# The feed-forward part of a two-layer encoder: inner features in three parts, and more of its products from half blocks

## The chip, the cores and the metric

The kernel runs on one core of one Trainium2 chip. The number that counts is the device time of one execution in microseconds. A core has a matrix engine (TensorE, PE in the profile; PEld is its weight load), an elementwise engine (VectorE, DVE), a scalar and activation engine (ScalarE, ACT), GpSimd (POOL), and SyncE (SP), whose queue issues most transfers from main memory.

## The reference

The program is an encoder of two layers over 512 tokens of 1024 features. The part of a layer that the change touches is the last line of the loop:

```python
    for layer in range(DEPTH):
        ...
        x = x + merged @ w_o[layer]
        h = rmsnorm(x, ffn_norm[layer])
        x = x + (jax.nn.silu(h @ w_gate[layer]) * (h @ w_up[layer])) @ w_down[layer]
    return rmsnorm(x, final_norm)
```

`w_gate` and `w_up` are 1024 x 2816, `w_down` is 2816 x 1024. The 2816 inner features are 22 blocks of 128.

## The kernel before

**Products in three.** All large products are made in a 32-bit format of reduced precision (`F32R`), with each float32 operand split into a rounded value `hi` and the rest `lo`. `mm3` (L207 to L210) adds hi x hi, hi x lo and lo x hi into one bank. A weight is split by `wsplit`: ACT casts (L92 as the profile names it) and DVE subtracts (L81). The results live in `hi` and `lo` tiles of 1024 columns, three of each (`hp`). The raw weight comes through `wload` (L193) into two buffers `raw` of 1 MB.

**Features across partitions.** xT (the residual stream) and hh/hl (the two halves of the normed input) hold features on the 128 partitions, 8 tiles of 512 tokens each. One block of 128 inner features is 8 x 3 = 24 matmuls of 512 columns into one bank `m`, times rbc (the rms scale of each token) on the way out. The blocks go in 11 pairs: gate block and up block of the pair, silu (gate) x up, split into gh/gl, which hold all 22 blocks.

**Seven products.** For 7 of the 11 pairs (blocks 4 to 17) the up pair is made by `seven`: the 256 outputs by 512 tokens by 1024 features of two blocks are cut in halves in each direction, 2 x 2 x 2, and seven products of half blocks (12 matmuls of 256 columns each) take the place of eight, after the scheme of Strassen and Winograd. The mixed weights (`sw`, s1, s2, a21 in place) are made on DVE as the call goes, the mixed inputs once per layer by `combine`, into `com` and into the space of gh/gl that is not in use yet. The products arrive in banks `m` and `y` and are summed into `u` (`gu` in rows).

**Back to 1024 features.** After the 11 pairs come the products with `w_down`: in layer 0 two output tiles at a time, each 22 blocks of 3 matmuls in one bank, summed into xT and absorbed into the next layer's hh/hl; in layer 1 with tokens on the partitions, eight banks open at once and the blocks in the outer loop, after xT has been transposed (L990) for the final norm.

**What sets the order.** Each engine takes its instructions in the order written by the build. Pieces inside `urgent()` (a priority) are moved ahead of the rest on their engine as far as buffers allow, so that splits of the next block run while PE is at this one. A tile of a pool with few buffers makes its next writer wait for its last reader.

Of the kernel before, what the change touches and what calls it, by code (L numbers as in the profile page):

```python
# [18 lines left out]
P = 128  # L19
# [28 lines left out]
def kernel(  # L48
# [679 lines left out]
    for l in range(LAYERS):  # L728
# [106 lines left out]
        with tc.tile_pool(name=f"ffn{l}", bufs=2, reuse_waits="tile") as fp:  # L835
            gh = fp.tile([P, FC, T], F32R, name="gh", bufs=1)
            gl = fp.tile([P, FC, T], F32R, name="gl", bufs=1)
# [3 lines left out]
            own = [fp.tile([P, DC // 2, 2, T // 2], F32R, name=name, bufs=1) for name in ("comh", "coml")]  # L841
            half = lambda v: v.rearrange("p (h t) -> p h t", h=2)
            spare = [v[:, FC - 4:FC, :].rearrange("p k (h t) -> p k h t", h=2) for v in (gh, gl)]
            com = lambda part, i, k: (spare if i < 2 else own)[part][:, k, i % 2, :]

            def combine(k):

                ge, go = an[2 * k], an[2 * k + 1]
                (x11, x12), (x21, x22) = [[half(xT[:, c, :])[:, i, :] for i in range(2)] for c in (2 * k, 2 * k + 1)]
                d, e = [half(fp.tile([P, T], F32, tag=tag, name="com", bufs=1)) for tag in ("s1", "s2")]  # L850
                u, v, m, n = d[:, 0, :], d[:, 1, :], e[:, 0, :], e[:, 1, :]
# [9 lines left out]
            def pair_of(tag):  # L861
                return fp.tile([P, 2, T], F32, tag=tag, name="gu", bufs=1)

            def tile_of(raw):

                with urgent():
                    wh, wl = wsplit(raw)
                ps = mbank()
                for c in range(DC):
                    mm3(ps, wh[:, c, :], wl[:, c, :], hh[:, c, :], hl[:, c, :], c == 0, c == DC - 1)  # L870
                return ps

            def gate(s, raw):
                ps = tile_of(raw)
                with urgent():
                    tt(s, ps, rbc, ALU.mult)
                    return act(s, s, AF.Silu)

            def seven(rg, ru, f0):

                s, u = pair_of("gu0"), pair_of("gu1")
                quarter = u.rearrange("p f (h t) -> p (f h) t", h=2)
                blk = lambda i, j: ru.rearrange("p (k two) c -> p k two c", two=2)[:, :, j, i * P:(i + 1) * P]
                a11, a12, a21, a22 = blk(0, 0), blk(0, 1), blk(1, 0), blk(1, 1)
                s1, s2 = [fp.tile([P, T], F32, tag=tag, name="sw", bufs=1).rearrange("p (k c) -> p k c", c=P)
                          for tag in ("s1", "s2")]

                def two():
                    return [hp.tile([P, 1024], F32R, tag=tag, name=tag).rearrange("p (h k c) -> p h k c", h=2, c=P)
                            for tag in ("hi", "lo")]  # L890
# [7 lines left out]
                mixed = lambda i: lambda part, k: com(part, i, k)  # L898
                of = lambda v, h: lambda part, k: v[part][:, h, k, :]
# [12 lines left out]
                product(p1, lambda part, k: first[part][:, 2 * k, :], plain(0, 0))  # L912
                with urgent():
                    ACT.copy(quarter[:, 1, :], p1)
                product(b26[:, 0, :], lambda part, k: first[part][:, 2 * k + 1, :], plain(1, 0))
                with urgent():
                    third = two()
                    split_act(s1, third[0][:, 0], third[1][:, 0])
                    split_act(a22, third[0][:, 1], third[1][:, 1])
                product(b26[:, 1, :], of(second, 0), mixed(1))  # L920
                with urgent():
                    tt(quarter[:, 0::3, :], quarter[:, 1:2, :].to_broadcast([P, 2, T // 2]), b26, ALU.add)
                    tt(s2, a12, s2, ALU.subtract)
                    fourth = two()
                    split_act(s2, fourth[0][:, 0], fourth[1][:, 0])
                product(b57[:, 1, :], of(second, 1), mixed(2))
                product(b57[:, 0, :], of(third, 0), mixed(0))
# [3 lines left out]
                product(b34[:, 1, :], of(third, 1), mixed(3))  # L931
                product(b34[:, 0, :], of(fourth, 0), plain(1, 1))
# [3 lines left out]
                with urgent():  # L936
                    tt(s, s, rbc.unsqueeze(1).to_broadcast([P, 2, T]), ALU.mult)
                    tt(u, u, s, ALU.mult)
                    split_act(u, gh[:, f0:f0 + 2, :], gl[:, f0:f0 + 2, :])
                return silu  # L940

            for f0 in range(0, FC, 2):
                with urgent():
                    rg = wload(rows(w_gate[l], 0, DC, f0 * P, 256))
                    ru = wload(rows(w_up[l], 0, DC, f0 * P, 256))
                if 4 <= f0 < FC - 4:
                    last_silu = seven(rg, ru, f0)
                    continue
                s, u = pair_of("gu0"), pair_of("gu1")
                for i in range(2):  # L950
                    if f0 + i < DC // 2:
                        combine(f0 + i)
                    last_silu = gate(s[:, i, :], rg[:, :, i * P:(i + 1) * P])
                    ps = tile_of(ru[:, :, i * P:(i + 1) * P])
                    with urgent():
                        tt(u[:, i, :], ps, rbc, ALU.mult)
                        tt(u[:, i, :], u[:, i, :], s[:, i, :], ALU.mult)
                        split_act(u[:, i, :], gh[:, f0 + i, :], gl[:, f0 + i, :])
            with tc.issue_after(last_silu.ins):
                lnexp = ACT.preload_act_table_set("natural_log_exp_and_others")  # L960
            groups = [(0, 8), (8, 8), (16, 6)]
            if l < LAYERS - 1:
                nn = [vecs[:, V_ATT + 8 * (l + 1) + c:V_ATT + 8 * (l + 1) + c + 1] for c in range(DC)]
                for c0 in range(0, DC, 2):
                    ps = [mbank(), mbank()]
                    for k0, nk in groups:
                        with urgent():
                            raw = wload(rows(w_down[l], k0, nk, c0 * P, 256))
                        for j in range(2):
                            with urgent():  # L970
                                wh, wl = wsplit(raw[:, :, j * P:(j + 1) * P])
                            for k in range(nk):
# [98 lines left out]
```

## Time and profile before

| | |
|---|---|
| time of the kernel, median of 3 runs | 1609.79 us (1609.61 to 1610.27) |
| the profiled execution's own time, its span | 1612.3 us, 1610.6 us |
| granted clock of TensorE, mean | 0.998 |
| busy: PE, PEld, DVE, ACT | 1595.3, 1342.1, 1122.2, 814.2 us |
| data moved, mean rate | 142.63 MB, 89 GB/s |

The profile comes from one execution, 1612.3 us, of which the trace covers 1610.6. A matmul's listed duration is longer than the time to the next one's start, since they overlap; what a stream of them costs is read from start to start. An engine's busy time counts overlapped work once.

### The profile page before, as it was taken

Reading aid. Unit: us, or ns where it says so; the run is one execution under the profiler, and the core shown is the slowest. Engines: PE = TensorE matmul, PEld = TensorE weight load, DVE = VectorE, ACT = ScalarE, POOL = GpSimd, SP = SyncE. Lnnn points to the kernel's source line nnn. Section 1 sums busy time; section 2 is a strip of 40 time slices with the busy share of each in tenths; the row PEclk is TensorE's granted clock in tenths of the full one; section 3 lists DMA queues with packets and bytes.
Section 4 is the critical chain, followed back from the end, with each engine's and each line's share of the span. In section 5 each row is a group of like instructions: output and inputs, shape, how many; then the busy total and the mean of one; then the engine's idle time right before and its main releaser. Section 6 shows DMA issues by size and latency. Waiting matters only on the chain.

```text
span 1610.6 us, 20117 instructions
## 1 busy us (share of the span) xinstructions
PE 1595.3 (99%) x7977; PEld 1342.1 (83%) x7977; DVE 1122.2 (70%) x1827; ACT 814.2 (51%) x1292; POOL 8.0 (0%) x21
## 2 busy tenths in 40 slices
PE   9999999999999999999999999999999999999998
PEld 7788888887888999888888888888878899988886
DVE  8888968887676777533368789788876767774224
ACT  4666665686453344322255567676754534343213
POOL 1000000000000000000000000000000000000000
PEclk9999999999999999999999999999999999999999
DMA  5312212221322333322332221213122332242321
GB/s 190 105 53 79 79 53 79 78 80 36 122 81 77 105 105 105 107 90 98 99 104 79 79 79 61 71 55 103 53 79 79 105 105 89 96 128 95 105 84 73
DMA packets 118078, 142.63 MB, mean 89 GB/s; under 512 B 3168, under 2 KB 100704, under 8 KB 117984
## 3 DMA queue, kind: packets, MB, share of 16 engines
q1 hardware_dynamic: 117696, 141.05, 26.8%
q8 instruction: 63, 1.03, 0.3%
q10 hardware_dynamic: 288, 0.30, 0.1%
q14 instruction: 31, 0.25, 0.0%
HBM read 139.23 MB, written 2.10 MB: 88 GB/s over the span
## 4 chain that ended last, share of the span: by engine, by line
PE 85%; DVE 9%; ACT 4%; issue 1%; DMA 1%; SPq 0%; DVEq 0%; ACTq 0%
PE m L209 21%; PE m L210 21%; PE m L208 21%; PE y L210 3%; PE y L209 3%; PE y L208 3%; DVE lo L81 2%; PE sc L549 2%; DVE fl L81 2%; PE s L209 1%; PE s L208 1%; PE s L210 1%; PE qk L666 1%; ACT hi L92 1%; DVE z L81 1%
## 5 line engine op out<-in xcount | busy, mean ns | idle before, releaser
L92 ACT CAST hi<-raw 128x1024 fp32r<-128x1024 f32 (+2 forms) x288 | 274.5, 954 | 496.3 <-PE m L209 251.6
L81 DVE TENSOR_TENSOR lo<-raw,hi 128x1024 fp32r<-128x1024 f32 (+2 forms) x296 | 322.9, 1092 | 219.6 <-ACT hi L92 218.8
L208 PE MATMUL m<-hh,hi 128*128 128x512 f32 (+1 forms) x1048 | 404.4, 386 | 1.2 <-DVE hi L296 1.1
L210 PE MATMUL m<-hh,lo 128*128 128x512 f32 (+1 forms) x1048 | 403.9, 386 | 0.0
L209 PE MATMUL m<-hl,hi 128*128 128x512 f32 (+1 forms) x1048 | 403.6, 385 | 0.0
L208 PEld LDWEIGHTS m<-hh,hi 128*128 128x128 f32 x1048 | 197.5, 189 | 40.2 <-ACT sq L78 1.5
L210 PEld LDWEIGHTS m<-hh,lo 128*128 128x128 f32 x1048 | 197.0, 188 | 38.4 <-DVE lo L81 0.2
L209 PEld LDWEIGHTS m<-hl,hi 128*128 128x128 f32 x1048 | 197.1, 188 | 38.0
L208 PE MATMUL m<-hi,hh 128*128 128x512 f32 x256 | 101.7, 397 | 0.0
L209 PE MATMUL m<-lo,hh 128*128 128x512 f32 x256 | 101.1, 395 | 0.0
L210 PE MATMUL m<-hi,hl 128*128 128x512 f32 x256 | 100.9, 394 | 0.0
L81 DVE TENSOR_TENSOR gu<-m,rbc 128x512 f32<-128x512 f32 x60 | 41.3, 689 | 61.7 <-PE m L210 60.6
L78 ACT ACTIVATE fl<-fl 128x1024 f32<-128x1024 f32 (+1 forms) x56 | 48.5, 872 | 41.8 <-DVE fl L81 41.8
L210 PE MATMUL m<-gh,lo 128*128 128x512 f32 x176 | 68.5, 389 | 0.0
L208 PE MATMUL m<-gh,hi 128*128 128x512 f32 x176 | 68.5, 389 | 0.0
L209 PE MATMUL m<-gl,hi 128*128 128x512 f32 x176 | 68.5, 389 | 0.0
L210 PEld LDWEIGHTS m<-hi,hl 128*128 128x128 f32 x256 | 48.3, 189 | 9.6
L208 PEld LDWEIGHTS m<-hi,hh 128*128 128x128 f32 x256 | 48.3, 189 | 9.4
L549 PEld LDWEIGHTS sc<-fl 128*128 128x128 f32 x384 | 50.0, 194 | 7.3 <-issue 2.6
L209 PEld LDWEIGHTS m<-lo,hh 128*128 128x128 f32 x256 | 48.3, 189 | 9.3
L549 PE MATMUL sc<-fl 128*128 128x128 f32 x384 | 52.2, 279 | 1.9 <-DVE fl L81 1.8
L92 ACT CAST gh<-gu 128x512 fp32r<-128x512 f32 (+1 forms) x30 | 24.7, 822 | 56.6 <-DVE gu L81 56.5
(293 smaller groups left out, 3047.1 us busy)
## 6 DMA issues: line engine op xcount, KB each, us to landing
raw<-in_w_in_dram SPq DMA_DIRECT2D x46, 1024.0 KB, 5.0
raw<-in_w_gate_dram SPq DMA_DIRECT2D x22, 1024.0 KB, 5.1
raw<-in_w_up_dram SPq DMA_DIRECT2D x22, 1024.0 KB, 5.1
raw<-in_w_down_dram SPq DMA_DIRECT2D x19, 1024.0 KB, 4.8
raw<-in_w_o_dram SPq DMA_DIRECT2D x8, 1024.0 KB, 4.7
raw<-in_w_b_dram SPq DMA_DIRECT2D x4, 1024.0 KB, 4.9
raw<-in_w_a_dram SPq DMA_DIRECT2D x4, 1024.0 KB, 5.0
raw<-in_w_down_dram SPq DMA_DIRECT2D x4, 768.0 KB, 4.1
```

Source lines behind the costliest of these rows:

```text
L78: return ACT.activation(o, i, func, **kw)
L81: return DVE.tensor_tensor(o, a, b, op)
L92: return ACT.copy(hi, src), tt(lo, src, hi.bitcast(F32), ALU.subtract)
L208: PE.matmul(ps, lh, rh, start=start, stop=False)
L209: PE.matmul(ps, lh, rl, start=False, stop=False)
L210: PE.matmul(ps, ll, rh, start=False, stop=stop)
L549: mm = PE.matmul(ps[:, c], K[:, c], Q[:, c], start=True, stop=True)
L666: PE.matmul(ps[c], q2[:, c, tok], kb[:, c, :], start=False, stop=True)
```

## The change

- The 22 inner blocks come in three parts of 8, 8 and 6 (`parts`). gh/gl become tiles of 8 blocks, two of each in turn.
- The products of `w_down` with one part are written as a generator (`down`), which makes one output tile (8 x 3 matmuls) at a time. While the next part's gate and up pairs are made, `next(todo)` puts one or two of these tiles after each of them, and `summed_up` adds the tile to xT. Only the last part's 6 blocks come after all pairs: in layer 0 as tiles that are also absorbed, in layer 1 with tokens on the partitions as before, over 6 blocks instead of 22.
- `down` loads `w_down` into a buffer of its own, `rd`, of which there is one.
- `seven` is now a function of one weight and one output. It serves up for pairs from block 4 on (9 per layer), and gate for pairs from block 8 on (7 per layer); the other pairs are made by `eight`, two whole blocks.
- `com` gets space of its own, and `combine` splits its four results in one step of 1024 columns. Inside `seven`, two mixed weights lie side by side in one tile and are split in one step; the product with rbc is made once over 1024 columns, and so is silu.
- Outside the feed-forward part nothing changes.

The diff, cut to its core:

```diff
-            gh = fp.tile([P, FC, T], F32R, name="gh", bufs=1)
-            gl = fp.tile([P, FC, T], F32R, name="gl", bufs=1)
...
-            own = [fp.tile([P, DC // 2, 2, T // 2], F32R, name=name, bufs=1) for name in ("comh", "coml")]
+            com = [fp.tile([P, DC // 2, 4, T // 2], F32R, name=name, bufs=1) for name in ("comh", "coml")]
...
-                for i, src in enumerate((u, m, v, n)):
-                    split_act(src, com(0, i, k), com(1, i, k))
+                split_act(f, com[0][:, k], com[1][:, k])
...
+            def eight(raw, out):
+
+                for i in range(2):
+                    with urgent():
+                        wh, wl = wsplit(raw[:, :, i * P:(i + 1) * P])
+                    ps = mbank()
+                    for c in range(DC):
+                        mm3(ps, wh[:, c, :], wl[:, c, :], hh[:, c, :], hl[:, c, :], c == 0, c == DC - 1)
+                    with urgent():
+                        tt(out[:, i, :], ps, rbc, ALU.mult)
...
-                gate(s[:, 0, :], rg[:, :, 0:P])
                 with urgent():
-                    first = wsplit(ru[:, :, 0:P])
-                    second = two()
-                    tt(s1, a21, a22, ALU.add)
-                    tt(s2, s1, a11, ALU.subtract)
-                    split_act(s2, second[0][:, 0], second[1][:, 0])
-                    tt(a21, a11, a21, ALU.subtract)
-                    split_act(a21, second[0][:, 1], second[1][:, 1])
+                    first = wsplit(raw[:, :, 0:P])
+                    s = fp.tile([P, 2, DC // 2, P], F32, tag="sw", name="sw", bufs=1)
+                    s2, s3 = s[:, 0], s[:, 1]
+                    tt(s3, a11, a21, ALU.subtract)
+                    tt(a21, a21, a22, ALU.add)
+                    tt(s2, a21, a11, ALU.subtract)
+                    second = wsplit(s.rearrange("p h k c -> p (h k) c"))
...
                 with urgent():
                     tt(quarter[:, 1:3, :], quarter[:, 1:3, :], b34, ALU.add)
-                silu = gate(s[:, 1, :], rg[:, :, P:2 * P])
...
+                    tt(out, out, rbc.unsqueeze(1).to_broadcast([P, 2, T]), ALU.mult)
+
+            def down(part, k0, evac):
+
+                nk = part[0].shape[1]
+                for i in range(DC):
+                    if i % 2 == 0:
+                        with urgent():
+                            raw = fp.tile([P, 2048], F32, tag="rd", name="rd", bufs=1)[:, :nk * 2 * P]
+                            raw = raw.rearrange("p (k c) -> p k c", c=2 * P)
+                            load(raw, rows(w_down[l], k0, nk, i * P, 2 * P))
                     with urgent():
...
+                        wh, wl = wsplit(raw[:, :, i % 2 * P:(i % 2 + 1) * P])
+                    ps = mbank()
+                    for k in range(nk):
+                        mm3(ps, wh[:, k, :], wl[:, k, :], part[0][:, k, :], part[1][:, k, :], k == 0, k == nk - 1)
+                    with urgent():
+                        evac(i, ps)
+                    yield
+
+            def summed_up(i, ps):
+                return tt(xT[:, i, :], xT[:, i, :], ps, ALU.add)
+
+            parts, at = (8, 8, 6), 0
+            todo = iter(())
+            for n, nf in enumerate(parts):
+                part = [fp.tile([P, 8, T], F32R, tag=tag, name=tag, bufs=2)[:, :nf, :] for tag in ("gh", "gl")]
+                slots = [DC * (j + 1) // nf - DC * j // nf for j in range(nf)]
+                for f0 in range(0, nf, 2):
+                    f = at + f0
...
+                    for j, dst in enumerate((s, u)):
+                        if f < DC // 2:
+                            combine(f + j)
+                        (eight if f < (8, 4)[j] else seven)(raws[j], dst)
...
+                        for _ in range(slots[f0 + j]):
+                            next(todo, None)
+                if n < len(parts) - 1:
+                    todo = down(part, at, summed_up)
+                    at += nf
...
-                for c0 in range(0, DC, 2):
-                    ps = [mbank(), mbank()]
-                    for k0, nk in groups:
...
+                def residual_out(i, ps):
+                    summed_up(i, ps)
+                    absorb(i, nn[i], i == 0)
+
+                for _ in down(part, at, residual_out):
+                    pass
...
-                order = [(k, t, c0, 512) for k in range(FC - 3) for t in range(TC) for c0 in (0, 512)]
+                order = [(k, t, c0, 512) for k in range(nf - 3) for t in range(TC) for c0 in (0, 512)]
```

Three places show how the built order moves. The first is DVE inside one call of `seven`, from the sum of the second product (`gu<-gu,y`) on, in the kernel before (`lo` is the second half of a split, `raw` the weight as loaded, a name behind "waits" an engine or a load that the row waits for):

```order
L81 TENSOR_TENSOR gu<-gu,y 128x2x256 [waits DVE_49,PE_49]
L81 TENSOR_TENSOR lo<-raw,hi 128x1024 [waits PE_49,Activation_49]
L81 TENSOR_TENSOR gu<-gu,y 128x512 [waits DVE_49,PE_49]
L81 TENSOR_TENSOR gu<-gu,y 128x256 [waits DVE_49]
L81 TENSOR_TENSOR lo<-raw,hi 128x1024 [waits DMAHW7_49,PE_49,Activation_49]
L81 TENSOR_TENSOR gu<-gu,y 128x512 [waits DVE_49,PE_49]
L81 TENSOR_TENSOR sw<-raw 128x512 [waits DMAHW0_49]
L81 TENSOR_TENSOR sw<-sw,raw 128x512 [waits DVE_49]
L81 TENSOR_TENSOR lo<-raw,hi 128x1024 [waits Activation_49]
L81 TENSOR_TENSOR raw<-raw 128x4x128
```

And the same stretch of a gate call in the changed kernel, from the next call's first mixed weight (s3) on:

```order
L81 TENSOR_TENSOR sw<-raw 128x512 [waits DMAHW5_49,DVE_49]
L81 TENSOR_TENSOR gu<-gu,y 128x2x256 [waits PE_49]
L81 TENSOR_TENSOR raw<-raw 128x4x128 [waits DVE_49]
L81 TENSOR_TENSOR sw<-raw 128x512 [waits DVE_49]
L81 TENSOR_TENSOR lo<-rd,hi 128x1024 [waits DMAHW6_49,PE_49,Activation_49]
L81 TENSOR_TENSOR gu<-gu,y 128x512 [waits PE_49]
L81 TENSOR_TENSOR gu<-gu,y 128x256 [waits DVE_49]
L81 TENSOR_TENSOR lo<-raw,hi 128x1024 [waits PE_49,Activation_49]
L81 TENSOR_TENSOR gu<-gu,y 128x512 [waits DVE_49,PE_49]
L81 TENSOR_TENSOR lo<-sw,hi 128x1024 [waits Activation_49]
L81 TENSOR_TENSOR gu<-gu,rbc 128x1024 [waits DVE_49]
L81 TENSOR_TENSOR sw<-raw,sw 128x512 [waits DVE_49]
```

Between the sum of the second product and the next one now stand a sum of raw blocks (a21 in place) and s2, both for the next call, and the split of a down tile's weight (`rd`), where the next gate block's split stood, and behind the call's last sums come the rbc product over 1024 columns.

The second is PE at the end of layer 1's last product ahead of the transposes (`xt`), before:

```order
L208 MATMUL m<-hh,hi 128x512
L209 MATMUL m<-hl,hi 128x512
L210 MATMUL m<-hh,lo 128x512
L990 MATMUL xt<-ident,xT 128x128 x24
L208 MATMUL m<-hi,gh 128x512
L990 MATMUL xt<-ident,xT 128x128 x8
L209 MATMUL m<-lo,gh 128x512
```

And in the changed kernel:

```order
L208 MATMUL m<-gh,hi 128x512
L209 MATMUL m<-gl,hi 128x512
L210 MATMUL m<-gh,lo 128x512
L988 MATMUL xt<-ident,xT 128x128 x32
L208 MATMUL m<-hi,gh 128x512
L209 MATMUL m<-lo,gh 128x512
L210 MATMUL m<-hi,gl 128x512
```

The transposes stood behind the last up block (`hh`) with one product of `w_down` among them; now they stand behind the last tile that is added to xT (`m<-gh,hi`), all 32 in a row.

The third is SP's queue at the end of layer 0's feed-forward part, as a piece of the difference (rows with a minus are of before, with a plus of the change):

```order
-L193 DMA raw<-in_w_in_dram 128x8x256 x3
+L193 DMA raw<-in_w_in_dram 128x8x256
+L926 DMA rd<-in_w_down_dram 128x8x256
+L193 DMA raw<-in_w_in_dram 128x8x256
+L926 DMA rd<-in_w_down_dram 128x6x256 x4
+L193 DMA raw<-in_w_in_dram 128x8x256
```

The last loads of `w_down` now stand between loads of the next layer's `w_in`, and each waits for the one buffer `rd`.

## Rows read from the trace of the kernel before

**Rows 1.** The page: span, and busy time, share and count of each engine.
```profile
span 1610.6 us, 20117 instructions
...
PE 1595.3 (99%) x7977; PEld 1342.1 (83%) x7977; DVE 1122.2 (70%) x1827; ACT 814.2 (51%) x1292; POOL 8.0 (0%) x21
```

**Rows 2.** Waits of PE, whole program: engine, tile, releaser: us, times, longest.
```profile
PE st L502 <- ACT kt L497: 2.1, 1, 2.1
PE sc L549 <- DVE fl L81: 1.8, 3, 1.1
```

**Rows 3.** Windows: length, then PE, PEld, DVE, ACT, POOL busy, PEclk, DMA share, GB/s.
```profile
499.00:646.00 147.00, 147.00 (x927) 133.71 (x926) 110.13 (x142) 57.96 (x82) 0.00 (x0) 1.00 0.32 101
690.00:806.00 116.00, 116.00 (x513) 96.09 (x512) 39.34 (x44) 30.90 (x38) 0.00 (x0) 1.00 0.29 95
500.94:511.01 10.07, 10.07 (x85) 10.07 (x84) 5.89 (x9) 4.64 (x7) 0.00 (x0) 1.00 0.40 114
```

**Rows 4.** Timeline of PE, one call of `seven`: start us, duration us, line, operation.
```profile
500.94 0.28 PE L208 MATMUL m<-hh,hi 128*128 128x256 f32 x1
501.05 0.28 PE L209 MATMUL m<-hl,hi 128*128 128x256 f32 x1
...
506.69 0.28 PE L208 MATMUL y<-gh,hi 128*128 128x256 f32 x1
...
511.01 0.40 PE L208 MATMUL m<-hh,hi 128*128 128x512 f32 x1
...
521.92 0.28 PE L208 MATMUL m<-hh,hi 128*128 128x256 f32 x1
```

**Rows 5.** Instructions on tile y: count, least/median/longest ns, first and last start.
```profile
L208 PEld LDWEIGHTS y<-hh,hi x112: 192/192/192, 502.3 to 1430.5; 128*128 128x128 f32 x112
L208 PE MATMUL y<-hh,hi x112: 283/283/283, 502.4 to 1430.7; 128*128 128x256 f32 x112
```

**Rows 6.** Timeline of DVE in the same call and the next blocks.
```profile
507.85 1.23 DVE L81 TENSOR_TENSOR lo<-raw,hi 128x1024 fp32r<-128x1024 f32 x1 [1.71 <-ACT hi L92]
509.00 1.13 DVE L81 TENSOR_TENSOR gu<-gu,y 128x512 f32<-128x512 f32 x2
...
515.24 0.69 DVE L81 TENSOR_TENSOR sw<-sw,raw 128x512 f32<-128x512 f32 x1
515.85 1.22 DVE L81 TENSOR_TENSOR lo<-raw,hi 128x1024 fp32r<-128x1024 f32 x1
516.99 0.68 DVE L81 TENSOR_TENSOR raw<-raw 128x512 f32<-128x512 f32 x1
517.59 0.68 DVE L81 TENSOR_TENSOR gu<-m,rbc 128x512 f32<-128x512 f32 x1
```

**Rows 7.** Timeline of ACT in the same call.
```profile
506.77 1.05 ACT L92 CAST hi<-raw 128x1024 fp32r<-128x1024 f32 x1 [2.26 <-PE y L209]
```

**Rows 8.** Waits from 455 to 806 us: us in total, times, longest.
```profile
ACT hi L92 <- PE m L209: 121.5, 38, 4.6
DVE lo L81 <- ACT hi L92: 88.7, 46, 4.7
```

**Rows 9.** DMA issues: count, KB each, median us from issue to landing.
```profile
raw<-in_w_down_dram SPq DMA_DIRECT2D x19, 1024.0 KB, 4.8
...
raw<-in_w_down_dram SPq DMA_DIRECT2D x4, 768.0 KB, 4.1
```

**Rows 10.** Timeline of all engines at the transposes of layer 1.
```profile
1480.01 2.78 PE L990 MATMUL xt<-ident,xT 128*128 128x128 f32 x24
...
1480.98 1.06 ACT L992 COPY xt<-xt 128x512 f32<-128x512 f32 x2
...
1482.54 0.47 PE L208 MATMUL m<-hi,gh 128*128 128x512 f32 x1
...
1483.10 1.15 PE L990 MATMUL xt<-ident,xT 128*128 128x128 f32 x8
...
1484.00 0.48 PE L209 MATMUL m<-lo,gh 128*128 128x512 f32 x1
```

More of the change, by code (lines that the diff above doesn't have):

```diff
@@ L849, in combine @@
                 (x11, x12), (x21, x22) = [[half(xT[:, c, :])[:, i, :] for i in range(2)] for c in (2 * k, 2 * k + 1)]
-                d, e = [half(fp.tile([P, T], F32, tag=tag, name="com", bufs=1)) for tag in ("s1", "s2")]
-                u, v, m, n = d[:, 0, :], d[:, 1, :], e[:, 0, :], e[:, 1, :]
+                f = fp.tile([P, 4, T // 2], F32, tag="sw", name="com", bufs=1)
+                u, m, v, n = [f[:, i, :] for i in range(4)]
                 tt(u, x12, x11, ALU.subtract)
@@ L857, in combine @@
                 stt(n, x21, go, m, ALU.mult, ALU.subtract)
-                for i, src in enumerate((u, m, v, n)):
-                    split_act(src, com(0, i, k), com(1, i, k))
[L861 to L883, printed above, removed]
-                a11, a12, a21, a22 = blk(0, 0), blk(0, 1), blk(1, 0), blk(1, 1)
[L885 to L890, printed above, removed]
+                split_act(f, com[0][:, k], com[1][:, k])
@@ new lines, in pair_of @@
+            def pair_of(tag, bufs):
+                return fp.tile([P, 2, T], F32, tag=tag, name="gu", bufs=bufs)
+            def eight(raw, out):
[7 more added lines that the diff above has]
+                        tt(out[:, i, :], ps, rbc, ALU.mult)
@@ L892, in product, with seven @@
+            def seven(raw, out):
+                quarter = out.rearrange("p f (h t) -> p (f h) t", h=2)
+                blk = lambda i, j: raw.rearrange("p (k two) c -> p k two c", two=2)[:, :, j, i * P:(i + 1) * P]
+                a11, a12, a21, a22 = blk(0, 0), blk(0, 1), blk(1, 0), blk(1, 1)
                 def product(ps, w, right):
@@ L923, in seven @@
                     tt(s2, a12, s2, ALU.subtract)
[L924 to L927, printed above, removed]
+                product(b57[:, 1, :], lambda part, k: second[part][:, DC // 2 + k, :], mixed(2))
+                with urgent():
+                    fourth = wsplit(s2)
+                product(b57[:, 0, :], odd(third, 0), mixed(0))
                 with urgent():
@@ L930, in seven @@
                     tt(quarter[:, 3, :], quarter[:, 2, :], b57[:, 0, :], ALU.add)
-                product(b34[:, 1, :], of(third, 1), mixed(3))
-                product(b34[:, 0, :], of(fourth, 0), plain(1, 1))
+                product(b34[:, 1, :], odd(third, 1), mixed(3))
+                product(b34[:, 0, :], lambda part, k: fourth[part][:, k, :], plain(1, 1))
                 with urgent():
                     tt(quarter[:, 1:3, :], quarter[:, 1:3, :], b34, ALU.add)
-                silu = gate(s[:, 1, :], rg[:, :, P:2 * P])
@@ L936, in seven @@
[L936 to L954, printed above, removed]
-                    with urgent():
-                        tt(u[:, i, :], ps, rbc, ALU.mult)
-                        tt(u[:, i, :], u[:, i, :], s[:, i, :], ALU.mult)
-                        split_act(u[:, i, :], gh[:, f0 + i, :], gl[:, f0 + i, :])
+                    tt(out, out, rbc.unsqueeze(1).to_broadcast([P, 2, T]), ALU.mult)
@@ L959 @@
             with tc.issue_after(last_silu.ins):
                 lnexp = ACT.preload_act_table_set("natural_log_exp_and_others")
-            groups = [(0, 8), (8, 8), (16, 6)]
             if l < LAYERS - 1:
                 nn = [vecs[:, V_ATT + 8 * (l + 1) + c:V_ATT + 8 * (l + 1) + c + 1] for c in range(DC)]
-                for c0 in range(0, DC, 2):
-                    ps = [mbank(), mbank()]
-                    for k0, nk in groups:
[L967 to L972, printed above, removed]
-                                f = k0 + k
-                                mm3(ps[j], wh[:, k, :], wl[:, k, :], gh[:, f, :], gl[:, f, :],
-                                    f == 0, f == FC - 1)
-                    for j in range(2):
-                        with urgent():
-                            tt(xT[:, c0 + j, :], xT[:, c0 + j, :], ps[j], ALU.add)
-                            absorb(c0 + j, nn[c0 + j], c0 + j == 0)
@@ L1002 @@
                             if k % 2 == 0:
-                                raw = wload(rows(w_down[l], k, 2, 0, D))
+                                raw = wload(rows(w_down[l], at + k, 2, 0, D))
                             sp[k] = wsplit(raw[:, k % 2:k % 2 + 1, :])
```

35 lines of the change are left out of this document (22 added, 13 removed).

## The prediction

> **What bounds the kernel now.** I read the page's busy line first: PE is busy 1595.3 us of a span of 1610.6 [rows 1]. The reader should see that 99% leaves 15 us of idle PE in the whole program, so that time can come off only by giving PE less to do. The waits of PE over the whole program say the same: the longest wait named is 2.1 us, and none has anything to do with the feed-forward part [rows 2]. The windows then show the stretches that the change touches. In layer 0, 499 to 646 us is the seven pairs of inner blocks that use `seven`: PE 147.00 of 147.00 us, DVE 110.13, ACT 57.96, clock 1.00. From 690 to 806 us is the projection back (`w_down`): PE 116.00 of 116.00, but DVE only 39.34 [rows 3]. So PE is full in both, and DVE has 25% of its time free in the first and 66% in the second. Two questions decide: how much PE work goes away, and whether DVE and ACT, which must now serve both kinds of work at once, still bring every split operand in time.
>
> **The change part by part.**
>
> *More blocks in halves.* A call of `seven` is 7 products of 12 matmuls of 256 columns, 84 in all, and replaces two blocks of 24 matmuls of 512 columns. Its price stands in the PE timeline: first matmul at 500.94, the first matmul after it at 511.01, so 10.07 us, 119.9 ns each [rows 4]. The two whole blocks behind it run from 511.01 to 521.92, 10.91 us [rows 4]; in the steady stretch of 512-column matmuls, 116.00 us hold 512 or 513 of them [rows 3], which is 226.6 ns each at most and 10.88 us for 48. One replacement saves 10.88 - 10.07 = 0.81 us. Before, 7 pairs per layer use `seven` for up; after, up uses it for the 9 pairs from block 4 on and gate for the 7 pairs from block 8 on, 16 per layer. That is 9 more per layer, 18 in both: 18 x 0.81 = **-14.6 us**. The 10.91 against 10.88 is 0.03 us lost where a 512-column block follows a `seven`; there are 18 more such places: **+0.5 us** (at least 0; at most 0.1 each, 1.8).
>
> The 36 matmuls more per replacement each bring a weight load. Loads are listed with 192 ns each, longer than the 120 ns between two matmuls, and the matmuls with 283 ns [rows 5]. In a `seven` the load side is busy 10.07 of 10.07 us, with 84 loads [rows 3]: 84 x 192 ns would be 16.1 us in a row, so these overlap, and the cost of a `seven` already contains them. I take 0 extra. "Perfetto Trace Analysis" of the Trainium skill, section Identifying the Most-Contended Engine, speaks against this change: it wants TensorE judged by the busy share of weight loads and not of matmuls, and this change adds weight loads where they are at 100%. If each of the 648 further loads were paid in full at 192 ns on top, 124 us would be lost; the spacing of 119.9 ns says that they are not, and the measurement decides.
>
> *The sums of one part between the blocks of the next.* The products with `w_down` are the same number of 512-column matmuls, 3 x 8 x 22 per layer. They only stand elsewhere: in parts two and three, 7 pairs and so 14 calls of `seven` per layer, each call is followed by one tile of 24 matmuls (two of them by two tiles), 24 x 226.6 ns = 5.44 us each. Moving work that fills PE to a place where PE is full gives and costs **0**, if operands are ready. What is new is the work around it: 16 sums into xT more per layer (three partial sums per tile instead of one; in layer 1 none before), at 0.60 us of DVE each. The cover is the count for one steady pair (gate `seven`, tile, up `seven`, tile). PE: 2 x 10.07 + 2 x 5.44 = 31.0 us. DVE issues 12 instructions of 1024, 18 of 512 and 2 of 256 columns. From start to start, where it runs without a pause, 1024 take 1.14 us (515.85 to 516.99) and 512 take 0.60 (516.99 to 517.59); the 256 I put at 0.4, since two, of 512 and 256, show 1.13 together [rows 6]. Sum 13.7 + 10.8 + 0.8 = 25.3 us, 81% of PE's 31.0, where it was 110.13 of 147.00, 75% [rows 3]. ACT has ten casts of 1024 at 1.05 us [rows 7], two of 512, two copies and a silu, about 12.4 us. Neither is the bound on average.
>
> *Is each operand on time?* That is the weak step, because all split buffers (`hi`/`lo`, three of each) are shared by both kinds of work. In the window 455 to 806 ACT's casts wait 38 times for PE to free a buffer, 121.5 us in all, and DVE's `lo` waits 46 times for ACT, 88.7 us [rows 8]: splits are made at the last moment that a buffer allows, and yet PE never waits. The tightest chain that I can follow in the trace: PE passes 506.69, a buffer is free, ACT casts at 506.77 [rows 4, 7], DVE makes `lo` from 507.85 for 1.23 us, ready at 509.08 [rows 6]; PE needs this `lo` at its third matmul, 0.46 us after 511.01 [rows 4], 2.4 us later. After the change the same slot belongs to the down tile's split. By the order, DVE has the sum of the second product and two mixed weights of the next call (a21, s2) before it. With the row's durations I get the cast at 5.83 us after the start of the `seven`, `lo` from 6.9 to 8.1, needed at 10.5: 2.4 us again. The other splits of a pair come out with 3 to 5 us. The smallest margin is the first tile after gate block 8, where ACT's copy waits for the product u x s of the pair ahead: 1.1 to 1.4 us, once per layer. So **0**; the bounds are 0 and, were each of the 32 calls late by 0.2 us, +6.4.
>
> *Its own weight buffer.* `w_down` goes through one buffer `rd` of 1 MB instead of two `raw`. A load can be issued only when both tiles of the last one are split, and then takes 4.8 us, for the last part 4.1 [rows 9]. Two tiles and two calls lie between two loads, 31 us, so the load is some 9 us early; in the last part of layer 0 two tiles of 18 matmuls are 8.2 us, and three tiles lie between the split that frees the buffer and its next use, 4 us early. **0**. What SP has queued behind a waiting `rd` load is the next gate or up block, needed a call later, and the first `w_in` of the next layer, two of which are already in.
>
> *The smaller edits.* One split of 1024 per `combine` instead of four of 256, silu and rbc over 1024 instead of 512, and the `p1` copy, all lie on ACT and DVE under a full PE: 0, and what they would cost uncovered is below 1 us each. *The transposes.* Layer 1's 32 transposes of xT must now stand behind the last sum into xT. Before, the first starts at 1480.01, and PE is back to a full rate at 1484.00 with one matmul at 1482.54 between them, about 3.8 us net; it is ACT's copies, from 1480.98 at 0.53 us each, that free the banks for the last eight at 1483.10 [rows 10]. The last sum into xT starts 0.2 us after PE's last matmul and takes 0.7; the first transposes read chunks that are long ready and cover it. ACT's copies then set the pace as before: **0** (between -0.1 and, with a second cast ahead of the copies and a late sum, +2).
>
> *Sum:* -14.6 + 0.5 = -14.1 us. The profiled execution should go from 1612.3 (span 1610.6, the rest lies outside it) to about 1598.2 with a span of 1596.5; from the median of 1609.79 it gives **1595.7 us**.
>
> **The rivals.** Changes under 0.2%, 3.2 us, can't be told from none.
>
> *A: splits a little late.* DVE takes its queue in order, and each `lo` of a down tile stands behind a sum that waits for PE. If each of the 32 calls, 16 per layer, loses 0.2 us, the time is 1595.7 + 6.4 = 1602 us. For it: the buffers are already taken at the last moment [rows 8]. Against: 2.4 us of slack in the traced chain. Chance 0.09.
>
> *B: DVE becomes the bound, and the kernel is slower.* Place: the 14 mixed pairs. DVE's 25.3 us would have to exceed 31.0; the gain is used up at 31.0 + 14.1 / 14 = 32.0 us, that is with DVE's instructions 26% longer than the rows, or 6.7 us of its waits in each pair that can't be moved. At 30% over, 32.9 us, the price is 14 x 1.9 = 27 us, time 1622. For it: waits in order cost DVE 36.9 us of each 147 already, so 81% may be more than it looks. Against: these waits are for buffers, not for lack of time. Chance 0.05.
>
> *C: half the columns at half the price.* If a 256-column matmul cost half of a 512-column one, 113.3 ns, a `seven` would take 9.52 us, each replacement save 1.36, and the time be 1609.8 - 24.5 = 1585 us. The 14 calls of before are all spaced as the one shown [rows 4], so 0.01. "TensorE: Matmul & The Clock Gate" of the Trainium skill, section Back-to-back issue gap, gives 262 cycles for 256 columns and 518 for 512 as an isolated gap; an estimate by it is 109 and 216 ns and 21 us saved, and the trace has 119.9 and 226.6.
>
> *D: one buffer for `w_down` is too few.* If a load comes 1 us late in 3 to 7 of the 12 pairs of tiles in each layer, 6 to 14 us are lost, time 1602 to 1609. Against: 4 to 9 us of slack from the rows. Chance 0.02.
>
> **How the numbers follow.** The forecast has 0.83, its own range from 1594 (no loss at switches, a run's scatter) to 1599 (+1.8 - 0.5 at switches, +2 at the transposes). The range reaches up into A, and holds 8 in 10: 1593 to 1601. Faster by more than 0.2%: forecast, A, C and half of D, 0.93; same: the rest of D and a small B, 0.03; slower: B, 0.04.
>
> **What would show it.** Right: PE with 648 more matmuls and a busy time near 1581 us, waits of PE in the feed-forward part still near nothing, a `seven` still 10.07 us, each mixed pair near 31.0 us, DVE near 81% there. Wrong: PE waits named "DVE lo" or "ACT hi" at the first matmul of a down tile or of a call (A, B), at "DMA rd" (D), a pair above 31.5 us, or transposes above 5 us.

## The result

The changed kernel takes **1595.53 us** (median of 4 runs, 1594.79 to 1595.85) against 1609.87 us (median of 4) before: a ratio of 0.991 with a 95% interval of 0.9893 to 0.9927, 14.3 us less. The forecast was 1595.7 us, 14.1 less.

The page of the changed kernel, its span and busy time, as [rows 1] of before:

```profile
span 1593.8 us, 21547 instructions
...
PE 1579.5 (99%) x8625; PEld 1359.5 (85%) x8625; DVE 1256.3 (79%) x1953; ACT 842.1 (53%) x1264; POOL 8.3 (1%) x21
```

PE has 648 matmuls more (8625 against 7977) and 15.8 us less to do. The profiled execution took 1595.75 us, so span and time fell by 16.8 and 16.6 us, more than the medians. The reason is the profiled execution of before, which was 2.4 us above the median: its first feed-forward matmul starts at 451.29 us, that of after at 448.86, behind a program that nothing was changed in. Most of this stands at one place, the matmuls into `st` (L502): PE waits 2.1 us for them before [rows 2] and 1.2 after (see the list of waits below). Behind the longer wait the granted clock of before is 0.52, the lower of two levels, for 3.4 us; after has 1.00 there. The window of before, in the columns of [rows 3]:

```profile
78.30:81.70 3.40, 3.40 (x17) 3.30 (x16) 3.40 (x10) 0.50 (x1) 0.00 (x0) 0.52 0.03 7
```

What the change did is read from the feed-forward parts alone. Windows from their first to their last matmul, layer 0 and then layer 1, before:

```profile
451.29:805.56 354.27, 354.27 (x1840) 305.04 (x1838) 208.47 (x275) 130.42 (x185) 0.00 (x0) 1.00 0.31 99
1245.44:1595.61 350.17, 350.09 (x1836) 301.52 (x1835) 196.18 (x259) 127.05 (x184) 0.00 (x0) 1.00 0.29 95
```

And after, in the same order, followed by one mixed pair (gate call, tile, up call, tile) and one call of `seven`:

```profile
448.86:796.10 347.24, 347.24 (x2164) 314.63 (x2163) 275.50 (x338) 144.55 (x172) 0.00 (x0) 1.00 0.31 99
1235.89:1578.85 342.96, 342.96 (x2160) 311.15 (x2159) 263.64 (x322) 140.72 (x170) 0.00 (x0) 1.00 0.29 96
612.71:643.79 31.08, 31.08 (x217) 29.16 (x216) 26.46 (x32) 12.29 (x14) 0.00 (x0) 1.00 0.32 102
550.55:560.62 10.07, 10.07 (x85) 10.06 (x84) 8.72 (x13) 4.52 (x6) 0.00 (x0) 1.00 0.40 118
```

Layer 0 is 7.03 us shorter, layer 1 7.21, together 14.24 us. PE is busy in all of both, at full clock. A mixed pair is 31.08 us, a call still 10.07, as in [rows 3]. DVE's share of a mixed pair is 26.46 of 31.08, 85%.

The longest waits of PE over the whole program, after:

```profile
PE sc L549 <- DVE fl L81: 2.2, 4, 1.1
PE idle L266 <- DVE ones_r L119: 1.4, 1, 1.4
PE st L502 <- ACT kt L497: 1.2, 1, 1.2
```

None of these, nor of the shorter ones, lies in the feed-forward parts, as before [rows 2].

The PE timeline at the first interleaved tile (24 matmuls, `m<-gh`) and the first calls beside it:

```profile
545.09 0.40 PE L208 MATMUL m<-gh,hi 128*128 128x512 f32 x1
545.32 0.40 PE L209 MATMUL m<-gl,hi 128*128 128x512 f32 x1
545.55 0.39 PE L210 MATMUL m<-gh,lo 128*128 128x512 f32 x1
...
550.55 0.28 PE L208 MATMUL m<-hh,hi 128*128 128x256 f32 x1
550.67 0.28 PE L209 MATMUL m<-hl,hi 128*128 128x256 f32 x1
...
560.62 0.40 PE L208 MATMUL m<-gh,hi 128*128 128x512 f32 x1
```

A tile of 512 columns behind a call takes 5.46 us (545.09 to 550.55), 0.02 more than 24 x 226.6 ns; the pitch inside the call is 0.12 us, as in [rows 4].

The splits on which it hangs, ACT's cast and DVE's `lo` of a tile's weight (`rd`). First the cast in the call that begins at 550.55:

```profile
556.44 1.05 ACT L92 CAST hi<-rd 128x1024 fp32r<-128x1024 f32 x1 [2.27 <-PE y L209]
```

Then DVE, the first tile's `lo` and that of the call at 550.55:

```profile
543.04 1.22 DVE L81 TENSOR_TENSOR lo<-rd,hi 128x1024 fp32r<-128x1024 f32 x1
...
557.53 1.23 DVE L81 TENSOR_TENSOR lo<-rd,hi 128x1024 fp32r<-128x1024 f32 x1
```

In that call the cast comes 5.89 us after the start, `lo` is ready at 558.76, 8.21 us after it, and PE needs it at its third matmul, 0.46 us behind 560.62: 2.3 us to spare. The very first tile's `lo` is ready at 544.26 and needed at 545.55, 1.3 us to spare. The casts of a call still wait for PE to free the buffer, as in [rows 7, 8], and none of that reaches PE.

Layer 1's transposes, as [rows 10], on all engines:

```profile
1550.51 3.78 PE L988 MATMUL xt<-ident,xT 128*128 128x128 f32 x32
1550.52 1.05 ACT L92 CAST hi<-raw 128x1024 fp32r<-128x1024 f32 x1 [3.81 <-issue]
...
1551.47 4.00 ACT L990 COPY xt<-xt 128x512 f32<-128x512 f32 x8
...
1554.05 0.48 PE L208 MATMUL m<-hi,gh 128*128 128x512 f32 x1
```

They are done in 3.54 us (1550.51 to 1554.05) instead of 3.76 without the one matmul between them: ACT's copies run in one piece of eight behind one cast, and the sum into the last xT chunk is not seen.

The loads of `w_down`, as [rows 9]:

```profile
rd<-in_w_down_dram SPq DMA_DIRECT2D x16, 1024.0 KB, 5.1
...
rd<-in_w_down_dram SPq DMA_DIRECT2D x4, 768.0 KB, 4.5
```

### The profile page after: what moved, and what is told of

It reads as the page before. It is cut to its first block, busy times and chain, and to the rows that moved or that the text cites. A ratio compares the mean times of both kernels' runs of the same rounds, so it can differ in the third digit from the quotient of the medians.

```text
span 1593.8 us, 21547 instructions
## 1 busy us (share of the span) xinstructions
PE 1579.5 (99%) x8625; PEld 1359.5 (85%) x8625; DVE 1256.3 (79%) x1953; ACT 842.1 (53%) x1264; POOL 8.3 (1%) x21
## 4 chain that ended last, share of the span: by engine, by line
PE 86%; DVE 9%; ACT 4%; issue 1%; DMA 0%; SPq 0%; DVEq 0%; ACTq 0%
PE m L209 20%; PE m L210 20%; PE m L208 20%; PE y L209 6%; PE y L208 6%; PE y L210 6%; DVE fl L81 2%; DVE lo L81 2%; PE sc L549 1%; PE qk L666 1%; DVE z L81 1%; PE wt L718 1%; PE po L600 1%; ACT hi L92 1%; PE qk L663 1%
## 5 line engine op out<-in xcount | busy, mean ns | idle before, releaser
L92 ACT CAST hi<-raw 128x1024 fp32r<-128x1024 f32 (+1 forms) x234 | 231.6, 991 | 337.3 <-PE m L209 231.5
L81 DVE TENSOR_TENSOR lo<-raw,hi 128x1024 fp32r<-128x1024 f32 (+1 forms) x242 | 274.1, 1134 | 67.7 <-ACT hi L92 66.8
L208 PE MATMUL m<-hh,hi 128*128 128x512 f32 (+1 forms) x832 | 312.4, 376 | 0.8 <-DVE hi L296 0.7
L209 PE MATMUL m<-hl,hi 128*128 128x512 f32 (+1 forms) x832 | 311.8, 375 | 0.0
L208 PE MATMUL y<-comh,hi 128*128 128x256 f32 x512 | 144.9, 283 | 0.0
L209 PE MATMUL y<-coml,hi 128*128 128x256 f32 x512 | 144.9, 283 | 0.0
L210 PE MATMUL y<-comh,lo 128*128 128x256 f32 x512 | 144.9, 283 | 0.0
L208 PEld LDWEIGHTS y<-comh,hi 128*128 128x128 f32 x512 | 98.3, 192 | 0.0
L209 PEld LDWEIGHTS y<-coml,hi 128*128 128x128 f32 x512 | 98.3, 192 | 0.0
L210 PEld LDWEIGHTS y<-comh,lo 128*128 128x128 f32 x512 | 98.3, 192 | 0.0
```

Of the source, the lines that this page charges most:

```text
L81: return DVE.tensor_tensor(o, a, b, op)
L92: return ACT.copy(hi, src), tt(lo, src, hi.bitcast(F32), ALU.subtract)
L208: PE.matmul(ps, lh, rh, start=start, stop=False)
L209: PE.matmul(ps, lh, rl, start=False, stop=False)
L210: PE.matmul(ps, ll, rh, start=False, stop=stop)
```

## The experiments

All are edits of the changed kernel; each is compared with the kernel before on the same chip (median 1609.8 to 1610.1 us).

**1. The tiles between the blocks, without more calls.**

```diff
-                        (eight if f < (8, 4)[j] else seven)(raws[j], dst)
+                        (eight if j == 0 or f < 4 or f > 16 else seven)(raws[j], dst)
```

> The parts and the tiles between the blocks as in the change, but halves only where they were before: up of the pairs from block 4 to 16, 14 calls of seven in both layers instead of 32. Theory (only the number of calls counts, the moved tiles are free): 18 x 0.81 - 0.5 = 14.1 us come back, and the time is that of the kernel before, 1609 to 1610 us, with no wait of PE in the feed-forward part. Rival (standing between the blocks is worth something by itself, by cover for the splits): clearly below, 1600 to 1606 us.

Measured: 1609.71 us, ratio 0.9998 (0.9989 to 1.0008). Layer 0's feed-forward part, from the first to the last matmul:

```profile
449.02:803.26 354.24, 354.24 (x1839) 305.02 (x1838) 217.31 (x257) 126.50 (x145) 0.00 (x0) 1.00 0.30 97
```

354.24 us, where before has 354.27. Moving the products with `w_down`, together with the smaller edits of the change, gives and costs nothing by itself; the gain is the 18 calls.

**2. All calls, the tiles behind a part's last pair.** PE has the same instructions, but the pairs have no tiles between them.

```diff
-                        for _ in range(slots[f0 + j]):
+                        for _ in range(DC if f0 + j == nf - 1 else 0):
```

> The same 32 calls of seven, but the eight tiles of a part come all behind the next part's last pair instead of one after each call. PE's work is the same to the instruction. Theory (the tiles are PE time in which DVE can catch up): a pair of two calls without tiles is 20.1 us of PE but 8 x 1.14 + 16 x 0.60 + 0.8 for the calls and 2.3 for product and split, 21.8 us of DVE; DVE is the bound, 1.7 us per pair in 14 pairs, 23 us, less some 2.4 us of slack at the start of each of 4 parts: 1609 to 1619 us, with waits of PE named DVE lo or ACT hi. Rival (DVE's in-order work is hidden wherever it stands, as only buffers limit it): 1595 to 1596 us.

Measured: 1645.23 us, ratio 1.0217 (1.02 to 1.0233), 50 us slower than the change and more than either theory said. PE's waits in part two and three of layer 0, and two windows: one pair from its last wait to the next, and the 3 us behind the wait:

```profile
PE y L208 <- ACT hi L92: 13.2, 7, 2.6
PE y L210 <- DVE lo L81: 0.4, 1, 0.4
```

```profile
594.53:618.94 24.41, 21.84 (x170) 21.62 (x169) 22.06 (x29) 9.88 (x12) 0.00 (x0) 0.93 0.27 87
597.38:600.40 3.02, 3.02 (x14) 3.00 (x14) 2.94 (x3) 0.89 (x1) 0.00 (x0) 0.51 0.00 0
```

DVE's 22.06 us in a pair is what the count gave (21.8), above PE's 20.1; but the pair takes 24.4. The timeline of PE shows where, at the third product of the up call:

```profile
594.41 0.28 PE L209 MATMUL y<-hl,hi 128*128 128x256 f32 x1
594.53 0.28 PE L210 MATMUL y<-hh,lo 128*128 128x256 f32 x1
597.38 0.58 PE L208 MATMUL y<-comh,hi 128*128 128x256 f32 x1 [2.57 <-ACT hi L92]
597.76 0.41 PE L209 MATMUL y<-coml,hi 128*128 128x256 f32 x1
597.97 0.41 PE L208 MATMUL y<-comh,hi 128*128 128x256 f32 x1
598.19 0.41 PE L209 MATMUL y<-coml,hi 128*128 128x256 f32 x1
```

ACT at that place (`gu<-gu` is silu over the gate pair):

```profile
595.34 1.06 ACT L78 ACTIVATE gu<-gu 128x1024 f32<-128x1024 f32 x1 [1.31 <-DVE gu L81]
596.30 1.03 ACT L92 CAST hi<-sw 128x1024 fp32r<-128x1024 f32 x1
```

And DVE, from the gate pair's product with rbc to the `lo` behind that cast:

```profile
594.08 1.22 DVE L81 TENSOR_TENSOR gu<-gu,rbc 128x1024 f32<-128x1024 f32 x1
595.22 0.69 DVE L81 TENSOR_TENSOR sw<-raw 128x512 f32<-128x512 f32 x1
597.36 1.23 DVE L81 TENSOR_TENSOR lo<-sw,hi 128x1024 fp32r<-128x1024 f32 x1 [1.46 <-ACT hi L92]
```

DVE, late by its count, makes the gate pair's rbc product at 594.08 and only then the mixed weight that the cast needs (595.22, done at 595.91); silu, which waits for the rbc product too, stands ahead of the cast in ACT's queue (595.34), and the cast starts at 596.30. PE waits 2.57 us. Behind the wait the matmuls start 0.21 us apart instead of 0.12, and the granted clock of those 3 us is 0.51, the lower of the two levels: 14 matmuls in 3.02 us that would have taken 1.7. So this pair loses the wait and 1.3 us more to the clock. Of the ten waits above 2 us in the whole program, eight have such a stretch beside them. The mean granted clock is 0.990 over 1641.3 us, 0.999 in the change: by an estimate from these two, some 15 of the 47 us between the two profiled executions are the clock's.

**3. Gate in halves from block 4 on**, in two pairs per layer that have no tiles to go with them.

```diff
-                        (eight if f < (8, 4)[j] else seven)(raws[j], dst)
+                        (eight if f < 4 else seven)(raws[j], dst)
```

> Gate uses seven from block 4 instead of 8, so two pairs of the first part in each layer, which have no tiles, are two calls in a row: 4 calls more, 36. By the count of PE alone: 4 x 0.78 = 3.1 us less, 1592.4 us. Theory (DVE is the bound in a pair without tiles): 1.7 us lost in each of these 4 pairs, less up to 2.4 us of slack per layer, so 1594 to 1599 us, with waits of PE on lo or hi in these pairs only.

Measured: 1601.14 us (profiled 1599.56), ratio 0.9942 (0.9928 to 0.9957): 4 calls more and 5.6 us slower than the change. The waits of PE there, and the window of the first part's four calls, the first gate call of part two and its tile:

```profile
PE y L208 <- ACT hi L92: 2.6, 2, 2.4
```

```profile
493.17:552.57 59.40, 56.80 (x445) 55.07 (x444) 56.54 (x71) 25.81 (x31) 0.00 (x0) 1.00 0.28 90
```

By count PE needs 5 x 10.07 + 5.46 = 55.8 us here and takes 59.4, with DVE busy for 56.54: 3.6 us lost per layer, some more than the theory's 3.3 at most, against 1.6 gained. The median lies above the theory's range, too: the three other runs, at 1600.64 to 1601.82 us, had a mean clock of 0.997 to 0.998 where the profiled one had 0.999.

**4. Four parts of 4, 6, 6 and 6 blocks**, so that every pair of two calls has tiles beside it.

```diff
-            parts, at = (8, 8, 6), 0
+            parts, at = (4, 6, 6, 6), 0
...
-                        (eight if f < (8, 4)[j] else seven)(raws[j], dst)
+                        (eight if f < 4 else seven)(raws[j], dst)
```

> Parts of 4, 6, 6 and 6 blocks, and gate and up both use seven from block 4 on, so each pair of two calls has tiles beside it: 36 calls, tiles of 4 or 6 blocks, 16 sums into xT more. DVE per pair 24.2 to 26.2 us against 25.6 to 32.4 of PE, 81 to 95%. Theory (free as long as DVE's count stays below PE's): 4 x 0.78 = 3.1 us less than the change, 1592.4 us, and no wait of PE in the feed-forward part. Rival (a tile must be long enough for each single split to be on time, and DVE at 95% in the second part is too tight): waits of PE in the second part, 1594 to 1600 us.

Measured: **1592.03 us**, ratio 0.989 (0.9874 to 0.9907); no wait of PE in the feed-forward part. Windows of part two (tiles of 12 matmuls), and of parts three and four:

```profile
492.47:574.83 82.36, 82.36 (x602) 78.48 (x600) 76.53 (x100) 36.27 (x45) 0.00 (x0) 1.00 0.33 106
574.83:759.00 184.17, 184.17 (x1287) 173.11 (x1286) 156.81 (x197) 74.67 (x90) 0.00 (x0) 1.00 0.32 104
```

PE is full at 82.36 us of part two with DVE at 93%. The same 36 calls as in experiment 3, 9 us faster: only what stands beside them differs. This version is faster than the change by 3.5 us, where the count gave 3.1.

**5. Two buffers for `w_down`**, on the four parts (gh/gl cut to tiles of 6 blocks to make room).

```diff
-                            raw = fp.tile([P, 2048], F32, tag="rd", name="rd", bufs=1)[:, :nk * 2 * P]
+                            raw = fp.tile([P, 2048], F32, tag="rd", name="rd", bufs=2)[:, :nk * 2 * P]
```

> The four parts, with gh/gl cut to tiles of 6 blocks, and two buffers for the raw w_down instead of one. Theory (one buffer is early enough everywhere): 1592 us as with one. Rival (loads through one buffer are sometimes late): 1 to 3 us less.

Measured: 1592.15 us, ratio 0.9887 (0.9859 to 0.9916). One buffer is early enough in the four parts; in the change itself no run has two, but there PE never waits in the feed-forward parts.

**6. More work on DVE, first try.** Products of 512 columns behind each tile's sum, whose result nothing uses; 2, 4 and 6 of them.

```diff
+                tt(xT[:, i, :], xT[:, i, :], ps, ALU.add)
+                for _ in range(4):
+                    tt(scr, rbc, rbc, ALU.mult)
```

> The change, with two further products of 512 columns on DVE behind each tile's sum into xT (their result is used by nothing). At 0.60 us each a mixed pair's DVE goes from 25.3 to 27.7 us, 89% of PE's 31.0. Theory (DVE costs nothing as long as its sum in a pair stays under PE's): 1595 to 1596 us. Rival (the tightest split, 2.4 us of slack, or the 1.1 to 1.4 us of the first tile, decides): some 1 us in each layer at the first tile, 1597 to 1598 us.

> Four such products behind each tile: 30.1 us of DVE per mixed pair, 97%. Theory by the sum per pair: still 1595 to 1597 us. Rival by the slack of single splits: each tile's 2.4 us of extra DVE work takes the 2.4 us of the traced chain, so PE waits at most calls, 0.2 to 1 us at 28 calls, 1601 to 1623 us.

> Six such products behind each tile: 32.5 us of DVE per mixed pair, 105%. Theory: PE is held to DVE's 32.5 us per pair, 14 x 1.5 = 21 us, 1616 us, with waits of PE on lo and hi. Rival by the slack of single splits: 3.6 us of extra work less 2.4 of slack, 1.2 us at 28 calls, 34 us, 1629 us.

Measured: 1597.90, 1620.33 and 1623.02 us (ratios 0.9923, 1.0066 and 1.0079; intervals 0.9894 to 0.9952, 1.0043 to 1.0089, 1.005 to 1.0108). These numbers say nothing about the mixed pairs, since the products didn't stay where they were written. DVE's timeline with four, in the first call of part one, where there is no tile yet:

```profile
505.23 0.69 DVE L81 TENSOR_TENSOR sw<-raw 128x512 f32<-128x512 f32 x1
505.83 2.14 DVE L81 TENSOR_TENSOR scr<-rbc 128x512 bf16<-128x512 f32 x3
507.89 1.22 DVE L81 TENSOR_TENSOR lo<-sw,hi 128x1024 fp32r<-128x1024 f32 x1
```

They need only rbc, so the build's order took them early and packed them into part one's calls and the start of part two; with four of them PE waited 12.9 us in the whole program at the casts, the longest time in calls without tiles again.

**7. More work on DVE, kept in place** by reading the chunk just summed.

```diff
-                    tt(scr, rbc, rbc, ALU.mult)
+                    tt(scr, xT[:, i, :], rbc, ALU.mult)
```

> As the two extra products per tile before, but they read the xT chunk just summed, so that DVE can't take them early: they stand inside the mixed pairs. DVE 27.7 us of 31.0 per pair, 89%. Theory (free as long as the sum in a pair stays below PE's): no wait of PE in the feed-forward part, 1595 to 1596 us. Rival (the tightest split decides, 1.1 to 1.4 us at the first tile): 1597 us or more.

> Four such products per tile: 30.1 us of DVE per mixed pair, 97%. Theory by the sum: 1595 to 1598 us. Rival by single chains, after what the runs without tiles showed (1.7 us too much by the sum, 3.4 us lost per pair, the clock's fall included): a wait in most of the 14 pairs, 1600 to 1630 us.

> Six such products per tile, read from the chunk just summed: 32.5 us of DVE per mixed pair, 105% of PE's 31.0. Theory by the sum: each of the 14 mixed pairs takes 32.5 us, 21 us more, 1616 us, less some us by which DVE is ahead at the start of each part. Rival by single chains and the clock that falls after a wait: twice that, 1630 us or more.

Measured: 1595.54, 1595.72 and 1609.96 us (ratios 0.9908, 0.991 and 1.0001; intervals 0.988 to 0.9937, 0.9881 to 0.9938, 0.999 to 1.0013). The four mixed pairs of part two with four products per tile:

```profile
551.25:675.57 124.32, 124.32 (x865) 116.65 (x864) 120.64 (x160) 48.31 (x57) 0.00 (x0) 1.00 0.31 102
```

And with six, followed by that kernel's waits of PE from 545 to 765 us:

```profile
550.61:679.91 129.30, 126.89 (x865) 117.29 (x864) 127.71 (x172) 49.06 (x57) 0.00 (x0) 1.00 0.30 98
```

```profile
PE y L208 <- ACT hi L92: 2.6, 7, 0.8
PE y L210 <- DVE lo L81: 0.7, 1, 0.7
```

At 97% of DVE PE does not wait once; with six DVE is full (127.71 of 129.30), PE waits in steps of at most 0.8 us at the casts, the clock stays up, and the four pairs take 5 us more. Over all, 14.4 us are lost where the sum gave up to 21. So in the mixed pairs the sum over a pair decides, to within a few per cent. The slack of the single splits was hardly touched: the products went into pauses of DVE, and in layer 0 of the run with four each tile's `lo` is still ready at least 2.0 us before it is needed, that of the first tile 1.3 us, about as without them. One of them, ready at 559.55 and needed at 561.80:

```profile
558.33 1.22 DVE L81 TENSOR_TENSOR lo<-rd,hi 128x1024 fp32r<-128x1024 f32 x1
```

DVE work that really pushes one split back by its slack was not tried.

**8. Silu behind the cast**, in the kernel of experiment 2.

```diff
-                        if j == 0:
+                        if j == 1:
                             with urgent():
                                 last_silu = act(s, s, AF.Silu)
...
+                                if f >= 8:
+                                    behind(last_silu, mark)
```

(Silu is written after the up call instead of after the gate call; `mark` is the cast of the up call's second split, behind which ACT now takes silu.)

> The kernel with all tiles behind a part's last pair, and one thing more: ACT takes silu of the gate pair behind the cast of the up call's second split instead of ahead of it. There PE waited 2.6 us per pair for that cast, which stood behind silu, which stood behind DVE's rbc product over the gate pair. Theory (this chain across two queues is the loss): the wait shrinks by the 1.05 us of silu and the wait for rbc, so at least 14 to 20 us come back, 1620 to 1632 us. Rival (DVE's count alone, 21.8 us against 20.1 per pair, is the loss): a wait in the same place or the next, 1640 to 1645 us.

Measured: 1630.18 us, ratio 1.0124 (1.0094 to 1.0153), 15 us less than experiment 2. One pair, and the matmul that waits in it:

```profile
592.56:615.88 23.32, 20.89 (x170) 20.42 (x169) 21.97 (x29) 9.89 (x12) 0.00 (x0) 1.00 0.28 91
```

```profile
592.56 0.28 PE L210 MATMUL y<-hh,lo 128*128 128x256 f32 x1
595.06 0.39 PE L208 MATMUL y<-comh,hi 128*128 128x256 f32 x1 [2.22 <-ACT hi L92]
```

The time is the one that the chain theory gave, but not by its way: the wait at this place is 2.22 us instead of 2.57, so 0.35 us of it was silu's place in ACT's queue, and not 1.05. That is what the rows of experiment 2 allow: the mixed weight was done at 595.91, and the cast behind silu started at 596.30. The rest came back elsewhere, the larger part of it by the clock: it is 1.00 over the pair, where it was 0.93, and part three's three pairs take 65.4 us instead of 69.4. Over the whole program the mean clock is 0.995 of 1628.7 us, where experiment 2 had 0.990 of 1641.3; by an estimate from these, 8 of the 12.7 us between the two profiled executions are the clock's, and PE's waits at the casts fell from 26.7 to 21.7 us. But the clock did not stay up everywhere: the next wait, of 2.22 us as well, ends at 618.39 and has the lower level behind it:

```profile
618.39:621.39 3.00, 3.00 (x13) 2.98 (x14) 2.94 (x3) 1.85 (x2) 0.00 (x0) 0.50 0.00 0
```

Of the eight waits above 2 us in this run four have such a stretch beside them; why fewer than in experiment 2 stays open. The pair shown is 23.3 us with DVE busy for 21.97, 94%. The larger part of the loss without tiles stays, and most of it is DVE's: its count, which exceeds PE's 20.1 us, and another 1.3 us in this pair in which it waits itself.

## Why the prediction was right

**The term of the 18 calls** was -14.6 us with +0.5 for the switches. The two layers fell by 7.03 and 7.21 us, of which 0.22 in layer 1 belongs to the transposes; 7.0 per layer is 9 x 0.81 - 9 x 0.03. A call cost 10.07 us in every one of the places, beside a tile or beside blocks. Experiment 1 takes the 18 calls away and gets the time of before.

**The moved tiles at 0** were right: experiment 1 has them between the blocks and runs as before. What the prediction left out is that they are needed. It compared the mixed pair with nothing; without tiles the same calls are 50 us slower (experiment 2) or lose more than they gain (experiment 3), since two calls in a row ask 22 us of DVE in 20 us of PE, and some of the waits that follow bring the lower clock on top. The interleaving pays for nothing by itself and for the whole gain together with the second use of `seven`.

**The splits on time**: the chain was put at 5.83 to 8.1 us and 2.4 us of slack, and measured 5.89 to 8.21 and 2.3; the first tile was put at 1.1 to 1.4 and has 1.3. DVE's share of a pair came out too low, 81% against 85%: the count took 0.60 us for all instructions of 512 columns, but some follow one another at 0.64 to 0.73, mostly where one touches a tile that the one ahead has just read or written, and ahead of each pause an instruction is busy for its whole listed time (0.68 or 1.22 us). That experiment 7 then measured the counted 97% with four products is partly luck: 26.46 us and eight products of 0.60 would be 31.26, over PE's 31.08, but the products came to stand between the instructions that had followed one another slowly, which there start 0.60 us apart.

**Rival B** put the point from which DVE would be the bound at PE's 31.0 us per pair and the end of the gain at 32.0. Experiment 7 fits roughly: no loss at 97%, all of the gain lost where DVE's own count was 25.3 + 7.2 = 32.5 us, though by B's sum the loss there would have been 21 us and not 14.4. **Rival A**, splits late by some tenths at each call, was wrong: even with 2.4 us more of DVE work per tile no call was late. **Rival C** was wrong: the pitch is still 0.12 us, and so was the fear of weight loads paid on top. **Rival D** was wrong: PE waits for no load in the feed-forward parts, and in the four parts a second buffer changes nothing (experiment 5). Its 12 pairs of tiles per layer are right for layer 0 alone; layer 1 loads `rd` for 8. In the last part of layer 0 ACT does wait 6.45 us for one load, until 766.04; the `lo` made from it is ready at 767.87, and the tile that needs it starts at 771.61, some 4 us later, as predicted.

**The transposes** at 0 were -0.2. The sum of the prediction, 14.1 us, hit the median difference of 14.3; the small rest is within a run's scatter (1594.79 to 1595.85). One small slip: the chances for faster, 0.83, 0.09, 0.01 and half of 0.02, add up to 0.94 and not 0.93.

## What to carry to other kernels

A trade of fewer matmuls for more elementwise work is worth its full matmul saving only where the other engine's time in the same stretch stays below PE's. Count both per repeating unit, and if the unit fails, look for matmul work that asks little of the other engine and put it into the unit: here moved tiles that are worth nothing alone carried 32 calls, and smaller parts carried 36. Count DVE from start to start and add some per cent; up to 97% nothing was lost here, and at 105% by the count the whole gain.

## What the runs showed of the hardware

After a wait of 2.57 us PE's matmuls of 256 columns started 0.21 us apart instead of 0.12 for the next 3 us, at a granted clock of 0.51, so that a wait in a busy stretch cost 1.3 us more than itself (experiment 2). In the four pairs with waits of up to 0.8 us (experiment 7) the clock was 1.00.

Not every wait of this length had it. In experiment 2 the one of 2.58 us that ended at 621.80 was followed, but for a few, by matmuls at the usual pitch. In experiment 8, of two waits of 2.22 us at the same place of neighbouring pairs, the one ending at 595.06 was followed by a clock of 1.00 and the one ending at 618.39 by 0.50 for the next 3 us; and in the kernel before, the wait of 2.1 us that ended at 77.42 was followed by 0.52. So two waits of the same length can differ by 1.3 us in what they cost. What decides it was not tried.
